# Expert outputs of the last pairs summed by one-hot products in SBUF instead of by accumulating row scatters to DRAM

## The chip, the cores and the metric

The kernel runs on one core of a Trainium2 chip. The metric is the device time of one execution in microseconds (us). Before the change three runs gave 815.13 us as their median (812.78 to 815.39).

The core's engines each run an instruction stream of their own: TensorE (PE in the profile; PEld is its weight load), VectorE (DVE), ScalarE (ACT), GpSimdE (POOL) and SyncE (SP), which here only issues DMAs. Matrix products accumulate in PSUM banks of 128 x 512 f32. Transfers from DRAM run on 16 DMA engines, whoever issues them.

## The reference

One decoder layer over 512 tokens of width 1024: three token mixers (a causal pooling mixer, latent attention, attention into 256 memory tokens) merged by gates, then a mixture of experts and a final RMSNorm. The change lies in the experts and the end. Cut to that part:

```python
def hierarchical_moe(h, w_rg, b_rg, w_re, b_re, w_gate_e, w_up_e, w_down_e):
    ...                                  # top-1 group of 4, top-2 of its 8 experts, weights per token
    def run_block(args):
        toks, e = args
        xb = x_pad[toks]
        a = jax.nn.silu(xb @ w_gate_e[e]) * (xb @ w_up_e[e])
        return a @ w_down_e[e]           # 1024 -> 256 -> 1024
    yb = lax.map(run_block, (row_tok.reshape(n_blk, MOE_BLOCK), blk_e))
    y = yb.reshape(R, D) * row_w[:, None].astype(yb.dtype)
    out = jax.ops.segment_sum(y, row_tok, num_segments=T + 1)[:T]
    return out.reshape(B, S, D)
...
x = x + hierarchical_moe(h2, ...)
return rms_norm(x, final_norm_g)
```

All is float32. There are 32 experts, so 1024 choices of a token and an expert, 32 to an expert on average.

## The kernel before

The first 520 us or so compute the mixers and the router. They are the same in both kernels. Behind them comes the expert stage.

**Pairs and slots.** The 32 experts are taken in 16 pairs (class `Pair`, objects `PP[0]` to `PP[15]`). A pair has 128 slots, 64 (`CAP`) for each of its two experts, and a slot holds one token. `onehot` makes `P`, a 0/1 matrix of tokens by slots; `info` multiplies by it to get each slot's weight (`wt`), its row scale (`rs`) and its token number. An expert with more than 64 tokens sets `flag`, and a branch on it (`tc.If`) runs `overflow`; with the timed inputs the branch is not taken.

**A pair's work.** `fetch` gathers the pair's rows of x from a DRAM copy `xd` (GpSimdE, an indirect DMA). `turn_x` turns them by TensorE, and ScalarE copies them with a scale. `up(0)` to `up(7)` multiply by the gate and up weights; the two experts use the two column halves of the PE array at once. `up(7)` ends with Silu on ScalarE and a product on VectorE. `turn` transposes the 128 x 256 result. `down` multiplies by the down weights in two halves of 512 columns, weighs the rows by `wt` into a tile `y`, and adds `y`'s rows to a DRAM copy of x, `xo`, by an indirect DMA with `compute_op=add` (line 1145), once for each pair. Unused slots point past the end and are dropped.

**The order.** All engines follow one hand-written list of steps for each pair (`SEQ0` for the first, `SEQM`, `SEQL` for the last): U is `up`, x `turn_x`, t and D are the turn and the `down` of the pair before, o, j and f prepare a pair three ahead. I call D(n) the down product of pair n; it stands in the list of pair n + 1.

**The weights.** 192 pieces of 512 KiB (twelve to a pair) are loaded by SyncE into a ring of 40 buffers made of tiles of several tags (`e`, `r`, `wh`, `wl`, `m`, `ac`; the three places of `m` are filled by two DMAs of 256 KiB each). A piece is issued when the one 40 back is used, and not before the DMA eight back has landed. In the list of the last pair the down weights of pair 14 come before the gate and up weights of pair 15, and the down weights of pair 15 last.

**The end.** In pair 14's list (`R`) `ACC` (all 512 rows, four tiles of 128) and `xa` (the rows of pair 14's slots) are read from `xo` behind the scatter of pair 13. `all_rows` norms `ACC` and writes it to the output; the rows of pairs 14 and 15 are not complete there. The rows of pair 14's slots (`xa`) get its product, are normed and written over by slot. For pair 15 the order is longer: its rows can be read (`rows_in(xs, q.ix)`, line 1258) only when the scatter of pair 14 is done; then its own product is added, and the normed rows are written over the output by slot (line 1353). The branch for `overflow` (line 1334) stands between the turn and the down product of pair 15.

Of the kernel before, what the change touches and what calls it, by code (L numbers as in the profile page):

```python
# [41 lines left out]
def trunk_and_moe(ctx, tc, a, out):  # L42
# [1018 lines left out]
    class Pair:
        def __init__(self, p, cd, inf, wts=None):
            self.cd, self.inf, self.wts, self.xe = cd, inf, wts, []
            self.XG = XG[p % 2]
# [42 lines left out]
        def info(self):  # L1107
# [6 lines left out]
            self.it, self.rs, self.wt = it, it[:, 8:9], it[:, 9:10]  # L1114

        def up(self, k):
# [5 lines left out]
            if k == KD - 1:  # L1122
                self.a = ut((128, 512))
                s.activation(self.a[:, 0:256], gu[:, 0:256], AF.Silu, scale=self.rs)
                v.scalar_tensor_tensor(self.a[:, 0:256], gu[:, 256:512], self.rs, self.a[:, 0:256], op0=OP.mult, op1=OP.mult)
# [8 lines left out]
        def down(self, xs=None):  # L1134
            y = ct2()
            for hf in range(2):
                hs = slice(hf * 512, (hf + 1) * 512)
                ps = self.down_half(hf)
                if hf:
                    v.tensor_scalar(y[:, hs], ps, self.wt, None, op0=OP.mult)  # L1140
                else:
                    s.activation(y[:, hs], ps, AF.Copy, scale=self.wt)
                if xs is not None:
                    v.scalar_tensor_tensor(xs[:, hs], ps, self.wt, xs[:, hs], op0=OP.mult, op1=OP.add)
            g.indirect_dma_start(out=xo[:, :], out_offset=bass.IndirectOffsetOnAxis(ap=self.ix[:, :1], axis=0), in_=y, in_offset=None,  # L1145
                                 bounds_check=T - 1, oob_is_err=False, compute_op=OP.add)

        def down_half(self, hf):
            y = bank(PC, "y", 2)
            for k in range(2):  # L1150
                for b, r in enumerate(HALF):
                    pe.matmul(y[r], lhsT=self.aT[:, k, r], rhs=self.wts[b][8 + 2 * k + hf], start=k == 0, stop=k == 1)  # L1152
            return y

# [97 lines left out]
    def rows_in(dst, ix=None):  # L1252

        if ix is None:
            for t in range(4):
                g.dma_start(dst[:, t].rearrange("p a b -> p (a b)"), xo[t * 128:(t + 1) * 128])
        else:
            g.indirect_dma_start(out=dst, out_offset=None, in_=xo[:, :], in_offset=bass.IndirectOffsetOnAxis(ap=ix[:, :1], axis=0),
                                 bounds_check=T - 1, oob_is_err=False)

    def rows_out(src, ix):
        g.indirect_dma_start(out=out[0], out_offset=bass.IndirectOffsetOnAxis(ap=ix[:, :1], axis=0), in_=src, in_offset=None,  # L1262
                             bounds_check=T - 1, oob_is_err=False)

    def norm(x, f):
        s.activation(junk, x, AF.Square, accum_out=f[:, 0:1])
        s.activation(f[:, 1:2], f[:, 0:1], AF.Sqrt, bias=eps[:, 0:1], scale=1.0 / D)
        v.reciprocal(f[:, 2:3], f[:, 1:2])
        v.scalar_tensor_tensor(x, x, f[:, 2:3], gf, op0=OP.mult, op1=OP.mult)

    def all_rows():
        for t in range(4):
            x = ACC[:, t].rearrange("p a b -> p (a b)")
            norm(x, fs[:, t])
            sync.dma_start(out[0, t * 128:(t + 1) * 128], x)
# [4 lines left out]
    fs = cst.tile([128, 6, 4], F32, name="fs")  # L1280
    for p, q in enumerate(PP):
        q.wts = [W[2 * p], W[2 * p + 1]]
        last = p == NP - 1
        for op in (SEQ0 if p == 0 else SEQL if last else SEQM):
            n_ = int(op[1]) if len(op) > 1 else p + 3
            if op[0] == "U":
                q.up(n_)
                if n_ % 2:
                    used(2)
            elif op[0] == "X":  # L1290
# [3 lines left out]
            elif op[0] == "x" and not last:  # L1294
                PP[p + 1].turn_x(n_)
            elif op == "L":
# [14 lines left out]
            elif op == "D":  # L1311
                PP[p - 1].down(xa if last else None)
                used(4)
                if last:
                    rows_in(xs, q.ix)
            elif op == "R" and p == NP - 2:

                gf, xa, xs, o, junk = (wide() for _ in range(5))
                g.memset(xa, 0.0)
                g.memset(xs, 0.0)  # L1320
                g.dma_start(gf, a["final_g"].broadcast_to([128, D]))
                ACC = row_major()
                rows_in(ACC)
                rows_in(xa, q.ix)
            elif op == "N":
                all_rows()
                norm(xa, fs[:, 4])
                rows_out(xa, PP[p - 1].ix)
# [3 lines left out]
    s.activation(f[:, 0:1], eps, AF.Sqrt)
# [1 line left out]
    with tc.If(nc.values_load(flag[0:1, 0:1], min_val=0, max_val=1) > 0):
# [4 lines left out]
    order = tc.manual_schedule()
    order.__enter__()  # L1340
    hs = [slice(hf * 512, hf * 512 + 512) for hf in range(2)]
    for hf in range(2):
# [1 line left out]
        v.scalar_tensor_tensor(xs[:, hs[hf]], ps, q.wt, xs[:, hs[hf]], op0=OP.mult, op1=OP.add)  # L1344
# [3 lines left out]
    v.tensor_tensor(o[:, hs[0]], xs[:, hs[0]], gf[:, hs[0]], op=OP.mult)
# [3 lines left out]
    v.scalar_tensor_tensor(o[:, hs[1]], xs[:, hs[1]], f[:, 3:4], gf[:, hs[1]], op0=OP.mult, op1=OP.mult)  # L1352
# [93 lines left out]
```

## Time and profile before

| what | value |
|---|---|
| median of three runs | 815.13 us |
| the profiled execution: its time | 815.2 us |
| its span, first to last instruction | 813.4 us |
| granted TensorE clock, mean of the span | 0.983 |
| DMA packets, all queues | 167.26 MB |
| PE, DVE, ACT, POOL busy | 94%, 40%, 37%, 36% |

In a timeline row the columns are start and duration in us, engine, source line, operation, written tile <- read tiles, shape, a count where equal instructions follow each other, and in brackets the idle time before the first with what ended it. In a row of stretches there is for each engine the busy time with its instruction count, then the granted TensorE clock (1.00 is full), the busy share of the 16 DMA engines (it can read a little over 1) and the rate in GB/s. One f32 product of 128 x 512 is recorded as two PE records. PE's busy time counts pipelined matmuls with modelled ends, so PE can read as busy while it starves; its waits say more.

### The profile page before, as it was taken

To read this page: it belongs to the slowest core of one execution; us is meant where nothing else is said; L and a number is where in the kernel's file an instruction comes from. 1 tells how busy PE (TensorE), PEld (TensorE's weight loads), DVE (VectorE), ACT (ScalarE), POOL (GpSimd) and SP (SyncE) were. 2 spreads that over 40 slices of the span, in tenths; PEclk is the share of its full clock that TensorE was granted. 3 is DMA by queue.
4 is the path that set the end of the run, shared out by engine and by line. 5 is a ranking of instruction groups with operands and counts; after the bars stand their busy time and mean duration, and the time that the engine had idled before them with its cause. 6 is when DMAs were issued, how large, how long until landed. Compare 5 with 4: busy or idle time off the path is not lost. (4 is left out here: it accounts for less than half of the span.)

```text
span 813.4 us, 9903 instructions
## 1 busy us (share of the span) xinstructions
PE 764.9 (94%) x3629; PEld 512.6 (63%) x3631; DVE 329.3 (40%) x613; ACT 304.0 (37%) x625; POOL 290.3 (36%) x180
## 2 busy tenths in 40 slices
PE   7999999999999999999999999999999998999843
PEld 3778888888887888788888888653333333223200
DVE  5668792344364234677764522423111111100032
ACT  6253453343337353656543322213222232121142
POOL 3255676433332688312226544311121221110301
PEclk9999999999999999999999999999999999999985
DMA  6523333322221322111233499979999999999973
GB/s 221 178 104 104 109 114 141 118 90 79 72 84 31 118 88 71 46 46 56 79 132 130 155 338 342 358 233 355 398 367 403 391 374 378 378 348 393 398 281 127
DMA packets 54371, 167.26 MB, mean 206 GB/s; under 512 B 8396, under 2 KB 9548, under 8 KB 54320
## 3 DMA queue, kind: packets, MB, share of 16 engines
q1 hardware_dynamic: 45792, 149.14, 49.5%
q0 software_dynamic: 5936, 13.01, 5.5%
q10 hardware_dynamic: 2592, 4.46, 1.5%
q8 instruction: 29, 0.48, 0.2%
q14 instruction: 22, 0.18, 0.1%
HBM read 159.86 MB, written 15.20 MB: 215 GB/s over the span
## 5 line engine op out<-in xcount | busy, mean ns | idle before, releaser
L125 POOL TENSOR_TENSOR wl<-r,wh 128x1024 fp32r<-128x1024 f32 (+3 forms) x75 | 167.3, 2238 | 211.0 <-ACT wh L180 187.0
L1121 PE MATMUL gu<-e,u 128*64 128x512 f32 x336 | 92.3, 608 | 3.2 <-DMA e<-in_w_e 3.2
L180 ACT CAST wh<-r 128x1024 fp32r<-128x1024 f32 (+3 forms) x85 | 82.1, 972 | 33.5 <-PE mm L199 13.3
L1145 POOL DMA_INDIRECT xo<-y,ix x15 | 24.0, 1601 | 182.4 <-DVE ix L1079 126.3
L198 PE MATMUL mm<-g,wh 128*128 128x512 f32 x180 | 72.8, 405 | 0.0
L199 PE MATMUL mm<-g,wh 128*128 128x512 f32 x180 | 71.0, 395 | 0.0
L1104 ACT ACTIVATE u<-xe,PR 128x128 f32<-128x128 f32 x120 | 34.2, 368 | 67.6 <-PE xe L1100 67.5
L471 PE MATMUL mm<-box,wh 128*128 128x512 f32 x144 | 56.8, 394 | 0.9 <-ACT wh L180 0.9
L472 PE MATMUL mm<-box,wh 128*128 128x512 f32 x144 | 56.3, 391 | 0.0
L1140 DVE TENSOR_SCALAR y<-y,it 128x512 f32<-128x512 f32 x15 | 11.3, 750 | 110.9 <-PE y L1152 110.9
L201 PE MATMUL mm<-g,wl 128*128 128x512 f32 x180 | 53.5, 395 | 0.0
L1121 PEld LDWEIGHTS gu<-e,u 128*64 128x64 f32 x336 | 24.0, 136 | 39.6 <-issue 23.4
L1152 PE MATMUL y<-e,u 128*64 128x512 f32 x144 | 39.9, 602 | 6.0 <-DMA e<-in_w_e 5.4
L435 ACT ACTIVATE m<-s,st 128x256 f32<-128x256 f32 (+3 forms) x48 | 24.3, 508 | 54.6 <-DVE st L433 54.1
L201 PEld LDWEIGHTS mm<-g,wl 128*128 128x128 f32 x180 | 33.7, 187 | 8.4 <-POOL wl L125 0.2
L198 PEld LDWEIGHTS mm<-g,wh 128*128 128x128 f32 x180 | 34.0, 189 | 7.4
L199 PEld LDWEIGHTS mm<-g,wh 128*128 128x128 f32 x180 | 33.8, 188 | 7.2
L476 PE MATMUL mm<-box,wl 128*128 128x512 f32 x144 | 36.6, 389 | 0.0
L198 PE MATMUL mm<-box,wh 128*128 128x512 f32 x78 | 31.7, 406 | 0.3 <-DVE g L283 0.3
L471 PEld LDWEIGHTS mm<-box,wh 128*128 128x128 f32 x144 | 27.1, 188 | 6.7 <-ACT wh L180 1.3
L476 PEld LDWEIGHTS mm<-box,wl 128*128 128x128 f32 x144 | 27.0, 188 | 5.7
L199 PE MATMUL mm<-box,wh 128*128 128x512 f32 x78 | 30.4, 390 | 0.0
(354 smaller groups left out, 1561.1 us busy)
## 6 DMA issues: line engine op xcount, KB each, us to landing
e<-in_w_e SPq DMA_DIRECT2D x120, 512.0 KB
r<-in_w_in SPq DMA_DIRECT2D x37, 512.0 KB
ac<-in_w_e SPq DMA_DIRECT2D x16, 512.0 KB
r<-in_w_e SPq DMA_DIRECT2D x15, 512.0 KB
wh<-in_w_e SPq DMA_DIRECT2D x15, 512.0 KB
wl<-in_w_e SPq DMA_DIRECT2D x14, 512.0 KB
m<-in_w_e SPq DMA_DIRECT2D x24, 256.0 KB
r<-in_w_bpm SPq DMA_DIRECT2D x8, 512.0 KB
```

What stands on the lines that cost most here:

```text
L125: eng.tensor_tensor(lo, x, hi.bitcast(F32), op=OP.subtract)
L180: s.copy(hi[:, :cols], r[:, :cols])
L198: pe.matmul(ps, lhsT=lh, rhs=rh, start=start and i == 0, stop=False)
L199: pe.matmul(ps, lhsT=lh, rhs=rl, start=False, stop=False)
L201: pe.matmul(ps, lhsT=ll, rhs=rh, start=False, stop=stop and i == m - 1)
L435: s.activation(P[:, :w], S[:, :w], AF.Exp, bias=st4[:, 0:1], accum_out=st4[:, 1:2])
L471: pe.matmul(ps, lhsT=lh, rhs=rh, start=k == 0, stop=False)
L472: pe.matmul(ps, lhsT=lh, rhs=rl, start=False, stop=False)
L476: pe.matmul(ps, lhsT=ll, rhs=rh, start=False, stop=k == KD - 1)
L1104: s.activation(x[:, j], ps[:, j], AF.Copy, scale=PR[:, k:k + 1])
L1121: pe.matmul(gu[r], lhsT=self.xe[k // 4][:, k % 4, r], rhs=self.wts[b][k], start=k == 0, stop=k == KD - 1)
L1152: pe.matmul(y[r], lhsT=self.aT[:, k, r], rhs=self.wts[b][8 + 2 * k + hf], start=k == 0, stop=k == 1)
```

## The change

Pairs 0 to 8 (`SC = 9`) are added to `xo` as before. Behind the down product of pair 8, in the list of pair 9, `xo` is read back to SBUF as `ACC`, into the place where x stood before (tag `ac`), four DMAs of 512 KiB. From pair 9 on nothing is scattered:

- `down` writes the weighted rows as two float32r tiles, high part (ScalarE) and remainder (VectorE).
- `where` makes `PT`, the 0/1 matrix of slots by tokens, from the slots' token numbers (VectorE).
- `combine(i, q)`, i from 0 to 7, multiplies one tile of 128 tokens of `PT` by one half of both parts (two float32r products of 128 x 128 by 512, PSUM bank `xe` or the new bank `cb`) and adds the bank to that part of `ACC` (VectorE). The eight calls of a pair wait in `todo` and are taken at the eight `c` of `SEQM`: four behind its D, four in the next list. Those of pair 13 are finished ahead of the last pair's list, those of pair 14 behind it.

The branch for `overflow` moves from behind the last pair's turn to ahead of the last pair's list. For the last pair `rs * wt` takes the place of `rs` on the up half, so its down product comes weighted. Its rows of `ACC` are picked by products with `P` (eight f32 products of 128 x 128 by 512) into the same two PSUM banks in which its down product then accumulates. All rows of `ACC` are normed and written by SyncE, and the last pair's slots are normed out of PSUM and written over by one scatter, which waits for those four writes. `rows_in`, `rows_out`, `norm`, `all_rows` and `xa`, `xs` go. From its third turn on the ring of weights has 36 buffers, since the four of `ac` hold `ACC`.

```diff
     def place(i):
-        j = i % RING
+        j = i % RING if i < 2 * RING else (i - 2 * RING) % (RING - 4)
...
+        def where(self):
+            tk = cst.tile([128, 4], F32, tag="tk", name=nm("tk"), bufs=1)
+            v.tensor_scalar(tk, K[:, C_TILE:C_TILE + 4], self.it[:, 6:7], -1.0, op0=OP.subtract, op1=OP.mult)
+            self.PT = ut((128, 4, 128), F32R)
+            v.tensor_tensor(self.PT, toks, tk.unsqueeze(2).broadcast_to([128, 4, 128]), op=OP.is_equal)
...
-        def down(self, xs=None):
-            y = ct2()
+        def down(self):
+
+            y = self.y = [ct2()] if self.scattered else [ct2(F32R), ct2(F32R)]
             for hf in range(2):
                 hs = slice(hf * 512, (hf + 1) * 512)
                 ps = self.down_half(hf)
...
+                if not self.scattered:
+                    s.activation(y[0][:, hs], ps, AF.Copy, scale=self.wt)
+                    v.scalar_tensor_tensor(y[1][:, hs], ps, self.wt, y[0][:, hs].bitcast(F32), op0=OP.mult, op1=OP.subtract)
...
+    def combine(i, q):
+        t, hs = i // 2, slice((i % 2) * 512, (i % 2) * 512 + 512)
+        cb = bank(PC, "cb", 1) if i % 2 else bank(PC, "xe", 2)
+        for j in range(2):
+            pe.matmul(cb, lhsT=q.PT[:, t], rhs=q.y[j][:, hs], start=j == 0, stop=j == 1)
+        dst = ACC[:, t].rearrange("p a b -> p (a b)")[:, hs]
+        v.tensor_tensor(dst, dst, cb, op=OP.add)
...
-    SEQM = "o U0 U1 j U2 t U3 x0 D U4 n U5 x1 U6 f U7 R".split()
-    SEQL = "t D U0 U1 N U2 U3 U4 U5 U6 U7".split()
+    SEQM = "o U0 c U1 j c U2 c t c U3 x0 D n U4 w c U5 c x1 c U6 f c U7".split()
+    SEQL = "t D U0 U1 U2 U3 U4 U5 U6 U7".split()
...
+                if p == SC:
+                    ACC = row_major()
+                    for t in range(4):
+                        g.dma_start(ACC[:, t].rearrange("p a b -> p (a b)"), xo[t * 128:(t + 1) * 128])
+                if p > SC:
+                    todo += [lambda i=i, q=PP[p - 1]: combine(i, q) for i in range(8)]
...
+    ys = [bank(PC, "y", 2) for hf in range(2)]
+    for t in range(4):
+        x = ACC[:, t].rearrange("p a b -> p (a b)")
+        todo.pop(0)()
+        todo.pop(0)()
+        if t == 1:
+            q.turn()
+        for hf in range(2):
+            pe.matmul(ys[hf], lhsT=q.P[:, t].bitcast(F32), rhs=x[:, hs[hf]], start=t == 0, stop=False)
+        f = fs[:, t]
+        s.activation(junk, x, AF.Square, accum_out=f[:, 0:1])
+        s.activation(f[:, 1:2], f[:, 0:1], AF.Sqrt, bias=eps[:, 0:1], scale=1.0 / D)
+    for hf in range(2):
+        q.down_half(hf, ys[hf])
+    for t in range(4):
+        x = ACC[:, t].rearrange("p a b -> p (a b)")
+        v.reciprocal(fs[:, t, 2:3], fs[:, t, 1:2])
+        v.scalar_tensor_tensor(x, x, fs[:, t, 2:3], gf, op0=OP.mult, op1=OP.mult)
+        sync.dma_start(out[0, t * 128:(t + 1) * 128], x)
```

How this moves instructions is read from the two programs. **GpSimdE, from the scatter of pair 8 to the end, before** (`xo<-y` is a pair's scatter, `<-xd` a fetch):

```order
L1145 DMA xo<-y_5724,ix_5361 512x1024
L1084 DMA y_4607<-xd,ix_5770 128x1024
L1145 DMA xo<-y_5828,ix_5464 512x1024
L1084 DMA XB<-xd,ix_5872 128x1024
L1145 DMA xo<-y_5929,ix_5566 512x1024
L1084 DMA y_4607<-xd,ix_5973 128x1024
L1145 DMA xo<-y_6030,ix_5667 512x1024
L1084 DMA XB<-xd,ix_6074 128x1024
L1145 DMA xo<-y_6111,ix_5770 512x1024
L1145 DMA xo<-y_6171,ix_5872 512x1024
L1319 MEMSET e_6209 128x1024
L1320 MEMSET e_6210 128x1024
```

And the same engine **now**, from the same scatter to the branch:

```order
L1158 DMA xo<-y_5719,ix_5361 512x1024
L1341 DMA ACC_5743<-xo 128x1024 x4
L1087 DMA y_4607<-xd,ix_5774 128x1024
L1087 DMA XB<-xd,ix_5895 128x1024
L1087 DMA y_4607<-xd,ix_6032 128x1024
L1087 DMA XB<-xd,ix_6171 128x1024
L1290 DMA y_4607<-in_final_g 128x1024
L1295 TENSOR_LOAD flag
```

Five scatters between the fetches and the loads of `xo` behind them are gone, and the four reads of `xo` stand right behind pair 8's scatter, ahead of the fetch for pair 12. **TensorE, in the list of pair 12 behind D(11), now** (`gu` products are `up`, `cb` and `xe` from `y` are `combine`, `xe` from `XB` is `turn_x`):

```order
L1131 MATMUL gu_6052<-wl_5756,u_6021 64x512
L1131 MATMUL gu_6052<-m_5758,u_6021 64x512
L1174 MATMUL xe_6139<-y_6109,u_6000 128x512
L1174 MATMUL xe_6139<-y_6110,u_6000 128x512
L1131 MATMUL gu_6052<-wl_5756,u_6021 64x512
L1131 MATMUL gu_6052<-m_5759,u_6021 64x512
L1174 MATMUL cb_6151<-y_6109,u_6000 128x512
L1174 MATMUL cb_6151<-y_6110,u_6000 128x512
L1103 MATMUL xe_6155<-K,XB 128x128 x4
L1174 MATMUL xe_6165<-y_6109,u_6000 128x512
L1174 MATMUL xe_6165<-y_6110,u_6000 128x512
```

Before, only the `gu` rows and `turn_x` stood there. **TensorE behind the last `up` product, now**, the first two of four tiles (`y<-ACC,P` picks the last pair's rows):

```order
L1174 MATMUL xe_6694<-y_6653,u_6357 128x512
L1174 MATMUL xe_6694<-y_6654,u_6357 128x512
L1174 MATMUL cb_6698<-y_6653,u_6357 128x512
L1174 MATMUL cb_6698<-y_6654,u_6357 128x512
L1356 MATMUL y_6692<-ACC_5743,P_6050 128x512
L1356 MATMUL y_6693<-ACC_5743,P_6050 128x512
L1174 MATMUL xe_6706<-y_6653,u_6357 128x512
L1174 MATMUL xe_6706<-y_6654,u_6357 128x512
L1174 MATMUL cb_6710<-y_6653,u_6357 128x512
L1174 MATMUL cb_6710<-y_6654,u_6357 128x512
L1140 MATMUL at_6714<-K,u_6686 128x128 x2
L1356 MATMUL y_6692<-ACC_5743,P_6050 128x512
```

Before, only the turn, the branch and the eight down products of 64 x 512 stood between the last `up` product and the end; now the branch is past, and sixteen `combine` products and eight picking products come first.

More of the change, by code (lines that the diff above doesn't have):

```diff
@@ L693, in load @@
             i = ring["loaded"]
-            if i % RING == RING - 4 and upto < min(i + 4, len(pieces)):
+            if i == 2 * RING - 4 and upto < i + 4:
                 return
@@ L701, in used @@
         ring["used"] += n_
-        load(ring["used"] + RING)
+        load(max(min(ring["used"] + RING, 3 * RING - 4), ring["used"] + RING - 4))
     def proj_v(p, half, w):
@@ L1150, in down_half @@
+            if self.scattered:
+                g.indirect_dma_start(out=xo[:, :], out_offset=bass.IndirectOffsetOnAxis(ap=self.ix[:, :1], axis=0), in_=y[0], in_offset=None,
+                                     bounds_check=T - 1, oob_is_err=False, compute_op=OP.add)
+        def down_half(self, hf, y=None):
+            more = y is not None
+            if not more:
+                y = bank(PC, "y", 2)
             for k in range(2):
                 for b, r in enumerate(HALF):
-                    pe.matmul(y[r], lhsT=self.aT[:, k, r], rhs=self.wts[b][8 + 2 * k + hf], start=k == 0, stop=k == 1)
+                    pe.matmul(y[r], lhsT=self.aT[:, k, r], rhs=self.wts[b][8 + 2 * k + hf], start=k == 0 and not more, stop=k == 1)
@@ L1161, in trunk_and_moe @@
+    PP = [Pair(p, pairs(code)[:, :, p], None, scattered=p < SC) for p in range(NP)]
     for q in PP[:3]:
@@ L1242, in overflow @@
                     q.down()
+                    for i in range(8):
+                        combine(i, q)
     SEQ0 = "X0 b1 X1 b2 X2 U0 X3 U1 X4 U2 X5 U3 X6 U4 X7 U5 j0 o U6 j1 x0 U7 L x1 j2 j f".split()
-    SEQM = "o U0 U1 j U2 t U3 x0 D U4 n U5 x1 U6 f U7 R".split()
-    SEQL = "t D U0 U1 N U2 U3 U4 U5 U6 U7".split()
[L1252 to L1275, printed above, removed]
+    SEQM = "o U0 c U1 j c U2 c t c U3 x0 D n U4 w c U5 c x1 c U6 f c U7".split()
+    SEQL = "t D U0 U1 U2 U3 U4 U5 U6 U7".split()
+    todo = []
+    fs = cst.tile([128, 5, 4], F32, name="fs")
     def wide():
         return W0.tile([128, 2, T], F32, tag="e0", name=nm("e"), bufs=6).rearrange("p a b -> p (a b)")
-    fs = cst.tile([128, 6, 4], F32, name="fs")
     for p, q in enumerate(PP):
@@ L1283, in trunk_and_moe @@
         last = p == NP - 1
+        if p == NP - 2:
+            gf = XG[0]
+            g.dma_start(gf, a["final_g"].broadcast_to([128, D]))
+        if last:
+            while todo:
+                todo.pop(0)()
+            order.__exit__(None, None, None)
+            with tc.If(nc.values_load(flag[0:1, 0:1], min_val=0, max_val=1) > 0):
+                extra[0] = True
+                overflow()
+                extra[0] = False
+            order = tc.manual_schedule()
+            order.__enter__()
+            q.rw = fs[:, 0, 3:4]
+            v.tensor_tensor(q.rw, q.rs, q.wt, op=OP.mult)
         for op in (SEQ0 if p == 0 else SEQL if last else SEQM):
@@ L1295, in trunk_and_moe @@
                 PP[p + 1].turn_x(n_)
+            elif op == "w" and SC <= p < NP - 1:
+                q.where()
             elif op == "L":
@@ L1311, in trunk_and_moe @@
             elif op == "D":
-                PP[p - 1].down(xa if last else None)
+                PP[p - 1].down()
                 used(4)
[L1314 to L1328, printed above, removed]
```

53 lines of the change are left out of this document (22 added, 31 removed).

## The prediction

> **What bounds the kernel now.** The trunk is untouched, so I read the expert stage and the end. First the table of stretches:
>
> ```profile
> core 0: us, PE busy (x) PEld busy (x) DVE busy (x) ACT busy (x) POOL busy (x), PEclk, DMA share, GB/s
> 676.50:784.90 108.40, 91.07 (x323) 28.45 (x322) 8.64 (x23) 26.70 (x69) 16.77 (x16) 0.98 1.00 379
> 677.00:690.00 13.00, 10.65 (x44) 3.36 (x40) 1.89 (x4) 3.05 (x9) 2.63 (x2) 1.00 1.02 408
> 690.00:694.00 4.00, 4.00 (x16) 1.30 (x14) 0.54 (x4) 0.37 (x1) 0.00 (x0) 1.00 1.05 332
> 746.00:750.00 4.00, 3.65 (x15) 1.01 (x12) 0.00 (x0) 0.37 (x1) 0.00 (x0) 1.00 1.05 320
> 648.00:660.00 12.00, 11.91 (x58) 4.12 (x56) 1.90 (x4) 3.81 (x11) 2.63 (x2) 1.00 0.99 372
> 717.00:729.00 12.00, 11.69 (x47) 3.94 (x46) 1.29 (x3) 2.53 (x7) 2.63 (x2) 1.00 0.92 303
> ```
>
> The DMA engines are full (share 1.00) and move about 408 GB/s where only loads and gathers run. Then the timeline of PE, at products with down weights (L1152) and at the last `up`:
>
> ```profile
> 637.09 3.65 PE L1152 MATMUL y<-e,u 128*64 128x512 f32 x16
> 650.21 3.65 PE L1152 MATMUL y<-e,u 128*64 128x512 f32 x16
> ...
> 676.45 1.08 PE L1152 MATMUL y<-e,u 128*64 128x512 f32 x4
> 678.87 1.07 PE L1152 MATMUL y<-e,u 128*64 128x512 f32 x2 [1.34 <-DMA e<-in_w_e]
> ...
> 695.39 1.04 PE L1152 MATMUL y<-e,u 128*64 128x512 f32 x2 [0.34 <-DMA e<-in_w_e]
> ...
> 713.94 1.07 PE L1152 MATMUL y<-r,u 128*64 128x512 f32 x2
> ...
> 784.85 0.64 PE L1121 MATMUL gu<-r,u 128*64 128x512 f32 x1 [1.44 <-DMA r<-in_w_e]
> 785.33 0.59 PE L1121 MATMUL gu<-r,u 128*64 128x512 f32 x1
> 785.76 1.02 PE L1121 MATMUL gu<-r,u 128*64 128x512 f32 x2
> ```
>
> While the ring holds weights, a pair takes PE 650.21 - 637.09 = 13.1 us. At D(9), 676.45, the ring is empty; from there PE waits for weights and a pair takes 18.9, then 18.55 us. **Until the last `up` product ends at 785.76 + 1.02 = 786.8 (call it E), the DMA engines are the bound**, with about 5 us of a pair's time free on PE. Behind E come 26.6 us of a chain:
>
> ```profile
> 785.11 0.75 DVE L1144 SCALAR_TENSOR_TENSOR e<-y,it,e 128x512 f32<-128x512 f32 x1 [22.67 <-DMA e<-xo,ix]
> 787.10 0.15 DVE L1268 RECIPROCAL fs<-fs 128x1 f32<-128x1 f32 x1
> 787.28 1.64 POOL L1145 DMA_INDIRECT xo<-y,ix  x1 [15.78 <-DVE fs L1268]
> 788.49 0.16 DVE L1268 RECIPROCAL fs<-fs 128x1 f32<-128x1 f32 x1
> ...
> 795.09 1.04 POOL L1258 DMA_INDIRECT e<-xo,ix  x1 [6.17 <-DMA xo<-y,ix]
> ...
> 797.00 0.20 ACT L1332 ACTIVATE fs<-eps 128x1 f32<-128x1 f32 x1
> 797.30 0.18 PEld L1152 LDWEIGHTS y<-r,u 128*64 128x64 f32 x1 [2.42 <-ACTq L1334]
> ...
> 801.36 0.75 DVE L1344 SCALAR_TENSOR_TENSOR e<-y,it,e 128x512 f32<-128x512 f32 x1 [6.82 <-DMA e<-xo,ix]
> ...
> 805.62 0.75 DVE L1352 SCALAR_TENSOR_TENSOR e<-e,fs,e 128x512 f32<-128x512 f32 x1
> 807.18 1.00 POOL L1262 DMA_INDIRECT out_dram<-e,ix  x1 [7.18 <-DVE e L1352]
> ```
>
> A gather of rows lands at 785, the scatter of pair 14 leaves at 787, its rows come back at 801, the result is ready at 806.4, and its scatter and the end take 813.4 - 806.4 = 7.0 us.
>
> **The change: what leaves the DMA stream.** The scatters of pairs 9 to 13 fall between D(9) and E:
>
> ```profile
> L1145 POOL DMA_INDIRECT xo<-y,ix x7 | 11.2, 1601 | 102.7 <-DVE ix L1079 54.8 <-DVE y L1140 32.2 <-DVE fs L1268 15.8
> ```
>
> These seven from 663 us on are pairs 8 to 14; 8 stays and 14 comes behind E. What one costs the stream: in 108.4 us 379 x 108.4 = 41.1 MB moved. 67 pieces of 0.524 MB landed in that time, 35.1 MB; three gathers and `xa` at 64 rows of 4 KB (1024 choices over 16 pairs) are 1.05, `xo` 2.1, the gain 0.5. 2.35 MB are left, 0.47 a scatter: read and written. That is 0.47/0.408 = 1.15 us. Besides, the rate sinks about each: 690 to 694 loses 4 x (1 - 332/408) = 0.75 us. So 1.9 us each, 9.5 for five; bounds from the rows: 0.75 (the dip alone), and 2.5 (18.55 less the 16 us that twelve pieces and a gather take at 408). With `xa` gone (0.26 MB, 0.6 us) the last gate weights land **10.1 us earlier**. The four reads of `xo` move from 768 to about 677; the bytes are the same, so E doesn't move by them, but D(10) comes 2.1/0.408 = 5.1 us later and 1.9 earlier: 695.4 + 3.2 = 698.6.
>
> One thing is added. With 36 buffers the `m` places, half-size DMAs of which eight may be out, hold pieces 149 to 151 (before 153 to 155) and once more 185 to 187, the last three that `up` needs. Loading them before, the stream thinned: 717 to 729 loses 12 x (1 - 303/408) - 0.75 = 2.3 us, but 648 to 660 only 0.3. I take **1.3**, halfway, and keep both ends. So weights put E at 786.8 - 10.1 + 1.3 = 778.0.
>
> **What is added on PE, and its cover.**
>
> ```profile
> 482.53 0.39 PE L883 MATMUL mm<-a,wh 128*128 128x512 f32 x1
> 482.76 0.39 PE L884 MATMUL mm<-u,wh 128*128 128x512 f32 x1
> ...
> 538.79 1.16 PE L1093 MATMUL xe<-P,ACC 128*128 128x128 f32 x8
> ```
>
> A float32r product of this shape records 0.39 us but starts 0.23 after the one ahead, which is its cost; the upper bound is 0.39. A pair has sixteen: 3.7 us, and PE needs 13.1 + 3.7 = 16.8 a pair, where weights come every 18.55 - 1.9 = 16.65. **PE and DMA become level**; the cover is used up. From 698.6, D(13) is at 749.0. Then come 9.4 us of products (3.5 down, 3.5 `up`, 0.6 turn, 1.8 `combine`).
>
> ```profile
> L1144 DVE SCALAR_TENSOR_TENSOR e<-y,it,e 128x512 f32<-128x512 f32 x2 | 1.5, 746 | 22.7 <-DMA e<-xo,ix 22.7
> L1125 DVE SCALAR_TENSOR_TENSOR u<-gu,it,u 128x256 f32<-128x256 f32 x7 | 3.4, 483 | 23.6 <-ACT u L1124 23.6
> L1348 DVE TENSOR_TENSOR e<-e,e 128x512 f32<-128x512 f32 x1 | 0.7, 683 | 0.0
> L1269 DVE SCALAR_TENSOR_TENSOR ACC<-ACC,fs,e 128x1024 f32<-128x1024 f32 x4 | 5.1, 1285 | 0.1
> ```
>
> Ahead of the branch PE must let VectorE finish: Silu, its product (0.48) and four adds of 0.75 take 4.1 us, then the turn and copy 1.0. (Adds that wait hold PSUM banks; with two of `xe` and one of `cb` a bank is asked for again after two products of `up` or `turn_x`, 1.5 to 2 us, and an add takes 0.75.) The branch itself, before: ACT's last instruction ends at 797.20 and PE goes on at 797.30 behind it, so 0.1 us; the bound is 2.0, from PE's own turn that ended at 795.3. D(14) is at 749.0 + 14.6 = 763.6, and with 3.5 + 6.9 us PE would reach E at 774.0. Weights say 778.0: 4 us of slack. SyncE's part of the branch waits for all loads to land, but behind it stand only the output writes. VectorE's adds (8 x 0.75 a pair) and `where` (0.7) leave it half idle. The waiting reads of `xo` hold the fetch of pair 12 on POOL from 670 to about 679; it is used at 698.
>
> **The end.** Behind E: `combine` of a tile takes PE 0.9 us and VectorE 2 x 0.75; picking a half waits for its add and takes 0.86: two records that start 0.43 apart (785.33, 785.76), as for a product on half the columns. The nearest full-width rows, at 538.79, take 1.16/8 = 0.145 for a quarter of the width, weight load included, so the upper bound is 8 x 0.145 = 1.16 a product and +2.4 us for eight. Tile by tile the last add ends at E + 11.7, the last picking at 12.7, the down products at 16.1. VectorE norms four tiles at 1.39 (787.10 to 788.49): 17.2. Two products with the gain, the factor, the scale: 19.6. But the scatter also waits for the four writes:
>
> ```profile
> out_dram<-e,ix POOLq DMA_INDIRECT x2, 3.3
> ACC<-xo POOLq DMA_DIRECT2D x4, 512.0 KB, 10.0
> ```
>
> The last write leaves at 17.2; 0.26 MB landed in 3.3 us unloaded, 0.52 MB need 0.6 more: 21.1 (10.0 in a full stream is the upper end, but weights are gone then). With 0.4 us to start and 807.18 to 813.4 behind, the end is E + 27.7; before it was 26.6. **The tail is 1.1 us longer**, though two DRAM round trips have gone.
>
> **Sum.** 778.0 + 27.7 = 805.7 against a span of 813.4: -7.7. The profiled execution took 815.2, 1.8 more than its span, and the median is 815.13; so I forecast **807.5 us**.
>
> **A rule weighed.**
>
> ```profile
> 734.00:739.50 5.50, 5.43 (x15) 2.28 (x17) 0.00 (x0) 0.69 (x1) 0.00 (x0) 0.69 1.03 411
> 790.00:800.00 10.00, 3.39 (x10) 1.14 (x12) 4.43 (x7) 2.33 (x4) 2.05 (x2) 0.50 0.82 278
> ```
>
> The granted clock falls to half at the end of before, where PE is mostly idle, and also in the stage, behind waits of only 1.5 us. The Trainium skill (TensorE: Matmul & The Clock Gate, "What's actually happening") has the clock halve after an idle window of about 3.4 us; by that the new tail, whose longest gap is 1 us, stays at full speed and gains over the old one, which the sum already has. The trace at 734 shows a drop on less, so I keep the drop as a rival.
>
> **Rivals.**
> 1. *PE at half clock behind E* (the slower side). Place: the products behind E; condition: a drop in the starved last 8 us. Every PE step doubles, the down products end at E + 29.6, the result is ready 2.1 later, and with 7.0 behind it the end is 11 us later: 818.5. It decides from 10 us on, that is only if the half clock lasts nearly the whole tail. Against it: at 782 to 787, more starved, the clock was full. 7%; half as long, 811 to 814, 5%.
> 2. *PE becomes the bound*, `combine` costing its recorded 0.39: 19.4 a pair, D(13) at 756.8, with 2.7 more behind it E at 784.5, time 814; a part of this, or a longer stop at the branch, 811 to 814. Against it: the 0.23 between rows. 12%.
> 3. *The scatters hid in the stream*, and weights come no earlier: E stays, tail +1.1: 816.2. Against it: the dips at each scatter. 5%.
> 4. *Better*: little thinning at `m`, scatters at 2.5 us; PE's own 774.0 is then the floor: 774.0 + 27.7 + 1.8 = 803.5. 10%.
>
> The forecast itself, 804.5 to 811, gets 61%. Three tenths of a per cent, 812.7 to 817.6, is about what can be told from no change. Faster: 61 + 10 + 9 of the 17 between = 80%; the same 12; slower 8, nearly all rival 1. Range **803 to 814**, which the bounds of the scatter (0.75 to 2.5 us) also give.
>
> **What would show it.** D(10) at about 698.6 and then periods near 16.7; PE's waits from there nearly gone; E at 778; no dip at scatters; the second `m` epoch by a thinner stream just ahead of E; clock 1.00 behind E; the last `combine` add at E + 11.7 and the final scatter at E + 21.5, ended by a write's landing. I am wrong if E lies beyond 783, by PE rows without waits (rival 2) or with them (rival 3), or if the tail exceeds 31 us.

## The result and the profile after

| | before | after |
|---|---|---|
| median of five runs | 813.10 us (812.42 to 815.39) | 807.81 us (805.84 to 810.23) |
| the profiled execution: time, span | 815.2, 813.4 us | 807.81, 806.0 us |
| granted TensorE clock, mean of the span | 0.983 | 0.991 |
| DMA packets, all queues | 167.26 MB | 164.17 MB |
| PE, DVE, ACT, POOL share of the span busy | 94%, 40%, 37%, 36% | 97%, 45%, 38%, 34% |

The ratio after to before is 0.9928, 95% interval 0.9901 to 0.9954: faster by 0.7%, or about 5.9 us; the medians differ by 5.3. The forecast was 807.5 us, 7.6 below the 815.13 it started from. **The sum came out right by luck: two of its parts were wrong and cancelled**, as the trace shows. All medians and ratios leave out two executions in a slow state, one of e9 (1692.58 us) and one of before taken beside e9 to e11 (856.97 us).

The stretches of the trace of after that answer to those of before (columns as there: each engine's busy time, the granted clock, the DMA share, GB/s):

```profile
672.40:779.30 106.90, 102.30 (x408) 36.01 (x407) 44.70 (x81) 23.87 (x62) 6.85 (x9) 0.97 0.95 369
677.00:690.00 13.00, 11.68 (x44) 3.83 (x40) 6.54 (x12) 2.30 (x6) 1.72 (x2) 1.00 1.03 410
712.00:724.00 12.00, 12.00 (x55) 4.83 (x54) 5.76 (x11) 4.03 (x11) 0.00 (x0) 1.00 0.94 326
754.00:764.00 10.00, 8.80 (x36) 3.60 (x32) 6.97 (x12) 2.08 (x6) 0.00 (x0) 1.00 1.03 404
762.00:766.00 4.00, 1.46 (x5) 0.58 (x4) 2.00 (x4) 0.37 (x1) 0.00 (x0) 0.85 1.04 389
766.00:770.00 4.00, 3.96 (x10) 1.23 (x12) 0.00 (x0) 0.15 (x1) 0.00 (x0) 0.50 1.04 398
770.00:774.00 4.00, 4.00 (x17) 1.17 (x14) 1.50 (x2) 1.22 (x2) 0.00 (x0) 0.80 0.51 203
774.00:779.00 5.00, 5.00 (x26) 1.54 (x22) 0.00 (x0) 0.00 (x0) 0.00 (x0) 1.00 0.00 0
```

In the last two rows the stream ends: it is half empty from 770 on and moves nothing from 774 on, and PE works on without a pause. The timeline of PE and its weight loads (PEld) in the same trace, with the down products (L1167), a `combine` call (L1174), the turn (L1140) and the last `up` products (L1131):

```profile
672.39 1.08 PE L1167 MATMUL y<-e,u 128*64 128x512 f32 x4
696.00 4.33 PE L1167 MATMUL y<-e,u 128*64 128x512 f32 x15
696.70 0.36 PEld L1167 LDWEIGHTS y<-e,u 128*64 128x64 f32 x2 [0.50 <-DMA e<-in_w_e]
697.97 0.20 PEld L1167 LDWEIGHTS y<-e,u 128*64 128x64 f32 x4 [0.92 <-DMA e<-in_w_e]
715.05 0.64 PE L1167 MATMUL y<-r,u 128*64 128x512 f32 x1
732.55 3.65 PE L1167 MATMUL y<-e,u 128*64 128x512 f32 x16
750.05 3.65 PE L1167 MATMUL y<-e,u 128*64 128x512 f32 x16
762.77 0.73 PE L1174 MATMUL cb<-y,u 128*128 128x512 f32 x2 [0.70 <-DVE ACC L1176]
764.92 0.66 PE L1140 MATMUL at<-K,u 128*128 128x128 f32 x2 [1.42 <-DVEq L1295]
766.04 1.11 PE L1167 MATMUL y<-r,u 128*64 128x512 f32 x1 [0.46 <-ACT u L1142]
777.01 2.31 PE L1131 MATMUL gu<-m,u 128*64 128x512 f32 x9
```

E is 777.01 + 2.31 = 779.3, and no `up` product of the last pair waits for a DMA: **PE sets E, not the weights**, which were there some 5 us earlier (the stream's last four pieces are down weights, which no `up` product needs). Ahead of D(14) PE waits for an add, for VectorE's part of the branch (L1295) and for the turn's copy, and then runs at half clock: a product that records 0.59 us elsewhere records 1.11.

The end, from VectorE, GpSimdE and (third row) the chain of waits:

```profile
790.57 0.68 DVE L1176 TENSOR_TENSOR ACC<-ACC,cb 128x512 f32<-128x512 f32 x1
795.61 1.28 DVE L1365 SCALAR_TENSOR_TENSOR ACC<-ACC,fs,y 128x1024 f32<-128x1024 f32 x1
796.92 2.65 DMA out_dram<-ACC
800.44 1.02 POOL L1377 DMA_INDIRECT out_dram<-e,ix  x1 [59.74 <-DMA out_dram<-ACC]
```

The last add ends at E + 11.9, the norms at E + 17.6, the last write lands at E + 20.3, the scatter behind it leaves at E + 21.1, and the span ends at E + 26.7.

Set against the forecast, both counted from D(9), which is 676.45 before and 672.39 after:

| from D(9) to | forecast | after | off by |
|---|---|---|---|
| D(10) | 22.1 | 23.6 | +1.5 |
| D(13) | 72.6 | 77.7 | +5.1 |
| D(14) | 87.2 | 93.7 | +6.5 |
| E, by PE | 97.6 | 106.9 | +9.4 |
| E, by the weights | 101.6 | not later than about 102 | |
| end | 129.3 | 133.6 | +4.3 |

From D(9) on the forecast had 7.7 us of gain; the trace has 136.95 - 133.6 = 3.3. The rest of the profiled difference, 4.1 us, lies ahead of D(9), all of it ahead of D(0), where the change adds and removes nothing. In the time of the trace that the forecast was made against, E would lie at 676.45 + 106.9 = 783.4, beyond the 783 that the forecast had named as a sign of being wrong.

### The profile page after: what moved, and what is told of

Read it like the earlier page. It is cut to its first block, busy times and chain, and to the rows that moved or that the text cites. A ratio compares the mean times of both kernels' runs of the same rounds, so it can differ in the third digit from the quotient of the medians.

```text
span 806.0 us, 10157 instructions
## 1 busy us (share of the span) xinstructions
PE 779.0 (97%) x3741; PEld 524.1 (65%) x3743; DVE 365.8 (45%) x675; ACT 304.4 (38%) x626; POOL 276.8 (34%) x169
## 2 busy tenths in 40 slices
DMA packets 53509, 164.17 MB, mean 204 GB/s; under 512 B 7906, under 2 KB 9058, under 8 KB 53456
## 5 line engine op out<-in xcount | busy, mean ns | idle before, releaser
L1131 PE MATMUL gu<-e,u 128*64 128x512 f32 x336 | 88.8, 607 | 0.9 <-DMA e<-in_w_e 0.9
L198 PE MATMUL mm<-g,wh 128*128 128x512 f32 x180 | 71.9, 400 | 0.0
L199 PE MATMUL mm<-g,wh 128*128 128x512 f32 x180 | 70.2, 390 | 0.0
L471 PE MATMUL mm<-box,wh 128*128 128x512 f32 x144 | 56.8, 394 | 0.9 <-ACT wh L180 0.9
L472 PE MATMUL mm<-box,wh 128*128 128x512 f32 x144 | 56.3, 391 | 0.0
L1158 POOL DMA_INDIRECT xo<-y,ix x9 | 14.3, 1594 | 89.9 <-DVE ix L1082 79.7
L1131 PEld LDWEIGHTS gu<-e,u 128*64 128x64 f32 x336 | 20.4, 135 | 33.0 <-issue 26.1
L1167 PE MATMUL y<-e,u 128*64 128x512 f32 x160 | 38.9, 600 | 0.4 <-DMA e<-in_w_e 0.4
L198 PE MATMUL mm<-box,wh 128*128 128x512 f32 x78 | 31.7, 406 | 0.5 <-DVE g L283 0.5
L471 PEld LDWEIGHTS mm<-box,wh 128*128 128x128 f32 x144 | 27.1, 188 | 6.7 <-ACT wh L180 1.3
L1154 DVE TENSOR_SCALAR y<-y,it 128x512 f32<-128x512 f32 x9 | 6.8, 751 | 54.1 <-PE y L1167 54.1
L472 PEld LDWEIGHTS mm<-box,wh 128*128 128x128 f32 x144 | 27.1, 188 | 5.3
```

The source lines that it names most:

```text
L198: pe.matmul(ps, lhsT=lh, rhs=rh, start=start and i == 0, stop=False)
L199: pe.matmul(ps, lhsT=lh, rhs=rl, start=False, stop=False)
L471: pe.matmul(ps, lhsT=lh, rhs=rh, start=k == 0, stop=False)
L472: pe.matmul(ps, lhsT=lh, rhs=rl, start=False, stop=False)
L1131: pe.matmul(gu[r], lhsT=self.xe[k // 4][:, k % 4, r], rhs=self.wts[b][k], start=k == 0, stop=k == KD - 1)
```

## The experiments

One table for all runs. D(0) is the first down product; ahead of it the change adds and removes nothing.

| run | median, us (lowest to highest) | ratio to before, 95% | D(0) | D(0) to E | E to end | D(0) to end |
|---|---|---|---|---|---|---|
| before | 813.10 (812.42 to 815.39) | 1 | 558.0 | 228.8 | 26.6 | 255.4 |
| after | 807.81 (805.84 to 810.23) | 0.9901 to 0.9954 | 553.9 | 225.4 | 26.7 | 252.1 |
| e1 | 802.03 (801.36 to 802.38) | 0.9849 to 0.9882 | 555.3 | 219.6 | 24.6 | 244.2 |
| e2 | 803.41 (803.05 to 804.42) | 0.9868 to 0.9902 | 553.5 | 221.7 | 26.0 | 247.7 |
| e3 | 807.44 (803.77 to 808.29) | 0.9904 to 0.9944 | 553.6 | 224.8 | 26.7 | 251.5 |
| e4 | 808.23 (807.34 to 810.16) | 0.9930 to 0.9960 | 553.6 | 225.3 | 26.7 | 252.0 |
| e5 | 806.56 (805.48 to 808.00) | 0.9902 to 0.9947 | 555.3 | 221.4 | 27.1 | 248.4 |
| e6 | 806.26 (804.33 to 808.52) | 0.9892 to 0.9933 | 553.9 | 223.9 | 26.7 | 250.6 |
| e7 | 806.27 (804.05 to 810.06) | 0.9893 to 0.9932 | 558.0 | 220.0 | 30.4 | 250.3 |
| e8 | 803.06 (801.36 to 808.67) | 0.9855 to 0.9893 | 560.1 | 227.5 | 19.3 | 246.8 |
| e9 | 804.80 (801.88 to 806.07) | 0.9864 to 0.9935 | 553.5 | 219.8 | 26.7 | 246.6 |
| e10 | 799.36 (797.11 to 804.39) | 0.9791 to 0.9841 | 558.5 | 223.9 | 20.3 | 244.1 |
| e11 | 814.30 (one run) | | 557.1 | 228.5 | 26.9 | 255.4 |
| e12 | 813.08 (809.05 to 816.31) | 0.9977 to 1.0011 | 553.2 | 227.9 | 26.1 | 254.0 |

### What a scatter costs the stream (e1)

The kernel before, with the scatters of five pairs left out:

```diff
+            if self in PP[9:14]:
+                return
             g.indirect_dma_start(out=xo[:, :], ..., compute_op=OP.add)
```

> The kernel before, with the scatters of pairs 9 to 13 left out (their sums are missing in the output) and nothing put in their place. If a scatter costs the full DMA stream 1.9 us, as the prediction had it, E (the end of the last up product) comes 9.5 us earlier than in the kernel before and the time is 803 to 804.5 us. If only the dips cost (0.75 us each), 809.3. If the scatters hid in the stream, 813. The tail behind E keeps its 26.6 us by all three.

D(9), the last gate and up weights' wait, and the last `up` row in the trace of e1:

```profile
673.74 2.17 PE L1154 MATMUL y<-e,u 128*64 128x512 f32 x4
772.96 0.64 PE L1121 MATMUL gu<-r,u 128*64 128x512 f32 x1 [1.04 <-DMA r<-in_w_e]
773.87 1.02 PE L1121 MATMUL gu<-r,u 128*64 128x512 f32 x2
```

Here PE still waits for a DMA just ahead of E, so the stream sets it. D(9) to E takes 774.9 - 673.7 = 101.2 us, 110.3 in before, 110.1 in its second trace (e11) and 109.5 in e12, whose expert stage is the same: 8.4 to 9.2 us, **1.7 to 1.8 us a scatter**; 1.9 was forecast. The timed median fell by 10.9, to 802.03, below the 803 to 804.5 expected: the tail, which was expected to stay, is 2.0 us shorter. In it the last rows of `xo` are there 13.6 us behind E (14.6 in before), and the last down products run at full clock (at 0.50 in before); how much each is worth stays open.

### Who sets E in the changed kernel (e2, e6, e4)

```diff
-        for j in range(2):
-            pe.matmul(cb, lhsT=q.PT[:, t], rhs=q.y[j][:, hs], start=j == 0, stop=j == 1)
+        pe.matmul(cb, lhsT=q.PT[:, t], rhs=q.y[0][:, hs], start=True, stop=True)
```

> The kernel after, where combine multiplies the high part of y alone (the remainder part of the sums is left out): half of its products, the DMAs as they are. If PE sets E from D(10) on (the new theory, from the trace of after), PE has 8 x 0.27 = 2.2 us a pair less, E moves from 779.3 to where the weights allow it, 774 to 776, and the tail loses about 2 more: 801 to 803 us. If the weights set E, as the prediction had it, E stays and only the tail gains: 805.5 to 806.

Same DMAs, less PE work, and D(0) to E is 3.7 us shorter, the median 4.4 us lower. That is the first theory's result, though the median misses its range by 0.4; by the second E would have stayed. So PE sets E. Of the 3.7 us, 1.1 lie behind D(14), where the half clock lasted 3.5 us here and 6.9 in after; from D(10) to D(14) e2 is 4.2 us shorter, and its step to D(10) is 1.7 longer.

e6 and e4 are one number, `SC = 8` and `SC = 10`.

> The kernel after with SC = 8: one scatter less, eight combine calls more. Theory 1: PE starves between D(9) and D(11) (the stream sets those two) and is the bound only behind them. Then the 4.4 us of the added combine calls fall into that starved time, D(10) or D(11) comes one scatter (1.9 us) earlier, and so does E: 805.5 to 806.5 us. Theory 2: PE is the bound of the whole stretch; then E is 4.4 us later: 811 to 812.5. Theory 3: the weights set E: 806 too, but with PE waiting for DMA ahead of E.

> The kernel after with SC = 10: one pair more is scattered, one less combined. If PE sets E, PE has 4.4 us less to do and the stream one scatter more (about 1.9 us): E at 775 to 776.5, time 804 to 805.5 us. If the weights set E, E comes 1.9 us later: 809.5 to 810.

D(8), D(9), D(10) and D(11) in e6:

```profile
659.22 0.64 PE L1167 MATMUL y<-r,u 128*64 128x512 f32 x1
678.81 3.81 PE L1167 MATMUL y<-e,u 128*64 128x512 f32 x16
696.91 3.65 PE L1167 MATMUL y<-e,u 128*64 128x512 f32 x16
714.86 0.64 PE L1167 MATMUL y<-r,u 128*64 128x512 f32 x1
```

In after the first two steps take 13.2 and 23.6 us, here 19.6 and 18.1: the added `combine` work went into time in which PE starved, and D(13) lies 196.0 us behind D(0), in after 196.1. From 696.91 to 714.86, 17.95 us, is a pair with its eight calls where PE doesn't starve; without them it took 13.1, so a call costs 4.8 / 8 = **0.60 us**. (The pairs from D(11) on have no `info` step ahead and take 17.5.) The theory that PE is the bound of the whole stretch falls. The time, 806.26, is the one that the first theory gave, but not for its reason: the scatter's 1.9 us didn't come out ahead of D(13), since with eight more calls PE has little starved time left, and most of what E gained (1.2 of 1.5 us) came behind D(14), where the half clock lasted 3.5 us instead of 6.9. Neither e6's median nor e4's can be told apart from after's. e4 missed its 804 to 805.5: D(9) to D(10) fell to 18.5, but with the reads of `xo` a list later D(10) to D(11) rose to 25.5, and 44.0 us together are more than after's 42.7. **What `SC` moves between PE and the stream comes back on the other side.**

### The branch and the half clock (e3, e5, e7)

e3 puts the last four `combine` calls of pair 13 behind the branch:

```diff
-    SEQL = "t D U0 U1 U2 U3 U4 U5 U6 U7".split()
+    SEQL = "c c t c c D U0 U1 U2 U3 U4 U5 U6 U7".split()
...
-            while todo:
-                todo.pop(0)()
```

> The kernel after, where the last four combine calls of pair 13 stand behind the branch, two ahead of the turn and two behind it, where PE stood still. If PE sets E, the stop shrinks by about 2 us, and if the half clock behind the branch came from the stop, 3 more: E at 774.5 to 777, time 803 to 805.5 us. If the half clock does not depend on the stop, 805.5 to 806. If the weights set E, no change: 807.8.

PE behind the branch, and D(14), in e3:

```profile
764.10 0.84 PE L1174 MATMUL xe<-y,u 128*128 128x512 f32 x2 [1.95 <-DVEq L1293]
764.74 1.06 PE L1174 MATMUL cb<-y,u 128*128 128x512 f32 x2
767.86 0.66 PE L1167 MATMUL y<-r,u 128*64 128x512 f32 x1
```

A miss (803 to 805.5 expected, 807.44 measured). The stop is as long as before, since the first product behind the branch waits for VectorE too, and the half clock falls on the `combine` calls (1.06 us instead of 0.63). D(14) to E is 10.5 instead of 13.3 us, but D(9) to D(10) took 26.4 here, and E moved by 0.6.

e5 leaves the branch out:

> The kernel after without the branch for overflow (left out; it is not taken with these inputs). If the stop at the branch costs what the trace of after shows, the turn behind it comes 1.5 us earlier, and if the stop also set off the half clock (2.9 us in D(14) and the first up products), D(14) to E takes 10.4 instead of 13.3 us: E at about 775 in the time of the profile of after, 803.5 to 804.5 us. If the half clock comes from something else there, 806.3.

From D(13) to E it takes 24.9 us, 29.3 in after: 4.4 less, as much as expected, though not in the parts expected. The granted clock is 1.00 all the way, and the turn comes 3.0 us earlier instead of 1.5, since the last `combine` call with its 0.70 us wait no longer stands ahead of it; that call now runs among the products of D(14), and D(14) to E takes 12.2 us, not 10.4. The median fell by only 1.3 us; its D(0) is 1.3 us later than in after, which leads to e12.

e7 puts the branch between `up(3)` and `up(4)` of the last pair, with the calls of pair 13 around the turn:

> The kernel after with the branch between up(3) and up(4) of the last pair, where VectorE has nothing open, and the last four combine calls of pair 13 around the turn in its old place. If the stop came from VectorE being held by Silu and the product ahead of the branch, PE stands 1 us or less there and the clock stays full: D(14) 2.8 us earlier, E at 775 to 776, 803.5 to 804.5 us. If the branch itself stops PE for 2 us wherever it stands, with the half clock behind it, nothing is gained: 807 to 808.

D(0) to E is 5.4 us shorter than in after, more than expected. But the tail is 3.6 us longer, and the median, 806.27, lies between the two forecasts. PE in e7 behind the last `up`:

```profile
780.10 0.73 PE L1174 MATMUL xe<-y,u 128*128 128x512 f32 x2 [2.16 <-ACTq L1317]
781.62 3.35 PE L1355 MATMUL y<-ACC,P 128*128 128x512 f32 x4 [0.32 <-DVE ACC L1176]
```

The wait has only moved: `up` products pass behind the branch, the first product that reads another engine's work from ahead of it waits (ACTq L1317 is ScalarE's part of the branch), and the half clock comes behind that (3.35 us for what takes 1.98).

### The calls in twos (e9)

In the trace of after a `combine` call is dear on the way from one kind of product to the other. PE there, starts in the first column:

```profile
757.73 1.08 PE L1131 MATMUL gu<-e,u 128*64 128x512 f32 x4
758.74 0.73 PE L1174 MATMUL cb<-y,u 128*128 128x512 f32 x2
759.40 1.08 PE L1131 MATMUL gu<-e,u 128*64 128x512 f32 x4
760.41 0.73 PE L1174 MATMUL xe<-y,u 128*128 128x512 f32 x2
760.99 0.62 PE L1174 MATMUL cb<-y,u 128*128 128x512 f32 x2
761.45 0.62 PE L1174 MATMUL xe<-y,u 128*128 128x512 f32 x2
```

One call between two `up` steps takes 759.40 - 758.74 = 0.66 us, and the step ahead of it 1.01 where it takes 0.86 in a row; the second of two calls in a row takes 761.45 - 760.99 = 0.46, which is the forecast's 2 x 0.23.

```diff
-    SEQM = "o U0 c U1 j c U2 c t c U3 x0 D n U4 w c U5 c x1 c U6 f c U7".split()
+    SEQM = "o U0 c c U1 j U2 c c t U3 x0 D n U4 w U5 c c x1 U6 c c f U7".split()
```

> The kernel after with the same combine calls taken two by two (cc) instead of one between two up products. In the trace of after a combine call between up products takes 0.81 us of PE (0.15 on the way in, 0.66 on the way out), the second and third in a row 0.58 and 0.46: it is the change of kind that costs. If so, a pair takes 0.9 us less where PE is the bound (17.5 to 16.6 us from D(11) on), E comes 2.5 to 3 us earlier, 804.5 to 805.5 us. If a call costs the same wherever it stands, 807.8; if two in a row wait for VectorE's adds to free their banks, a pair takes more and the time is 808 to 810.

D(12), D(13), the call ahead of the branch, the turn behind it and D(14) in e9, then a stretch of it:

```profile
730.66 3.65 PE L1167 MATMUL y<-e,u 128*64 128x512 f32 x16
747.46 3.65 PE L1167 MATMUL y<-e,u 128*64 128x512 f32 x16
759.83 0.74 PE L1174 MATMUL cb<-y,u 128*128 128x512 f32 x2 [0.70 <-DVE ACC L1176]
761.98 0.41 PE L1140 MATMUL at<-K,u 128*128 128x128 f32 x2 [1.42 <-DVEq L1295]
762.86 0.64 PE L1167 MATMUL y<-r,u 128*64 128x512 f32 x1 [0.46 <-ACT u L1142]
```

```profile
762.00:766.00 4.00, 3.54 (x18) 1.30 (x20) 0.36 (x1) 1.06 (x2) 0.00 (x0) 1.00 1.03 375
```

A pair takes 16.8 us instead of 17.5: 0.7 us gained, 0.9 expected. And the stop at the branch has the same waits as in after to a hundredth (0.70, 1.42, 0.46), but **this time the clock stays at 1.00**. E comes 5.6 us earlier in the trace: 2.8 behind D(14), where the clock is full, the rest ahead of it, which is the 2.5 to 3 expected of the calls.

### All that helped together (e8, e10)

e8 is `SC = 8`, the branch of e7, and the eight calls of pair 14 among the `up` products of the last pair; e10 has `SC = 9`, the calls in twos, and no call close ahead of the branch (`B`):

```diff
+    SEQL = "c c t c c D U0 U1 c c U2 U3 B U4 U5 c c U6 c c U7 c c".split()
```

> The kernel after with SC = 8, the branch as in the run before, and the eight combine calls of pair 14 among the up products of the last pair instead of behind them (PE does them before E, so E comes 4.4 us later than without, but the tail loses 5 to 6 us, among it VectorE's adds that PE waits for, and its output writes leave earlier). By theory 1 of PE: 1.9 from SC, 3 from the branch, 1 to 2 from the tail, so 801 to 802.5 us. If E is held by the weights by then, the combine calls cost nothing ahead of E: 799 to 801. If neither the branch nor SC helps, 806 to 808.

> The kernel after with all that has helped: SC = 9, combine calls two by two, the last four of pair 13 around the turn, the branch between up(3) and up(4) of the last pair with no combine call close ahead of it (so VectorE and ScalarE have nothing open there), and the combine calls of pair 14 among the up products of the last pair. From the traces, D(0) to the end: 252.1 us in after, 246.8 in e8; 2.5 to 4 less than e8 by the calls in twos and a shorter stop at the branch, so 243 to 244.5 and a time of 799 to 800.5 us. If the stop at the branch or the half clock stay, 801 to 803.

PE behind the branch, the last pair's down products and the final scatter in e10:

```profile
778.02 0.70 PE L1174 MATMUL xe<-y,u 128*128 128x512 f32 x2 [0.49 <-PEq L1317]
790.47 3.65 PE L1167 MATMUL y<-e,u 128*64 128x512 f32 x16
797.02 1.02 POOL L1374 DMA_INDIRECT out_dram<-e,ix  x1 [51.67 <-ACT e L1372]
```

The stop is 0.49 us, the clock stays full, and the final scatter waits for its own rows and no longer for an output write. e10 takes **799.36 us, ratio 0.9816 (0.9791 to 0.9841)**: it beats both kernels, and time and stage (244.1 us from D(0)) are as expected. e8 was expected at 801 to 802.5 and took 803.06.

### What lies ahead of D(0) (e11, e12)

> The kernel before once more, unchanged, for a second trace of it. From D(0) to the end the first trace takes 255.4 us, and D(0) lies at 558.0, where the nine other traces have 553.5 to 560.1. If the expert stage repeats and the time ahead of D(0) is what varies, D(0) to the end is 255.4 within 0.7 us here, wherever D(0) lies. If the stage itself varies by some us, not.

255.4 again, with D(0) 1.0 us earlier: the expert stage of before repeats, and the time ahead of it varies. (e12, with the same stage, has 254.0.) One reason for the variation is on record in the granted clock: near 535 us it is halved for 3.5 us in before, e11, e7 and e10, for 6.9 us in e8, and not at all in the other traces. From the first product of L883 (L884 in the changed kernels) to D(0) it takes 94.9 to 95.1 us with the short stretch, 96.6 with the long one and 93.3 to 93.5 without. It comes and goes in kernels of either sort, and from run to run of one kernel the mean clock differs alike (e8: 0.987 in the traced run, 0.996 to 0.998 in the five others), so it doesn't come from the change.

> The kernel before with one more small constant tile (16 bytes a partition, one memset), which moves every tile behind the constants by 32 bytes of SBUF, as the tile tk of the change does. Ahead of D(0), which the change does not touch, the traces fall into two groups: between the first product of L550 and the first scores of the heads (L746 before, L747 after) 155.7 us in before, its second trace, e1 and e5; 154.1 to 154.2 in after and the other seven; and between L770 (L771) and L883 (L884) 115.5 against 114.6. Where the tiles stand splits them the same way: wh starts at byte 62400 in before and e1 and 62144 in e5, both multiples of 64, and at 62432 in after. If the place of the tiles sets the pace of the products there, this kernel shows 154.1 and 114.6 and takes 2.5 us less than before: 810.3 to 811.3. If it is something else in the program, 155.7 and 115.5, and 813.

```diff
     fs = cst.tile([128, 6, 4], F32, name="fs")
+    pad = cst.tile([128, 4], F32, name="pad")
+    v.memset(pad, 0.0)
```

The same float32r products in before, then in e12, and behind each the start of L746:

```profile
320.10 0.39 PE L199 MATMUL mm<-g,wh 128*128 128x512 f32 x1
320.33 0.40 PE L198 MATMUL mm<-g,wh 128*128 128x512 f32 x1
320.57 0.39 PE L199 MATMUL mm<-g,wh 128*128 128x512 f32 x1
...
330.18 0.39 PE L746 MATMUL s<-g,g 128*128 128x512 f32 x1
```

```profile
320.27 0.39 PE L198 MATMUL mm<-g,wh 128*128 128x512 f32 x1
320.50 0.39 PE L199 MATMUL mm<-g,wh 128*128 128x512 f32 x1
320.72 0.39 PE L198 MATMUL mm<-g,wh 128*128 128x512 f32 x1
...
327.73 0.39 PE L746 MATMUL s<-g,g 128*128 128x512 f32 x1
```

The products start 0.233 us apart in before and 0.227 in e12, and both stretches read 154.1 and 114.5 us, as in after. So **32 bytes in the place of the tiles change the pace of these products by 2.6%**, 2.5 us in all. But the median of e12, over twelve runs, is only 0.5 us below before's, within the interval of no change; the one trace is the fastest of the twelve. Part of the answer is the granted clock on record for each run: its mean is 0.983 over these twelve and 0.985 over the seventeen runs of before beside them. A straight line through time against clock for both, an estimate, puts e12 1.6 us below before at the same clock (standard error 0.5). Why these runs had the lower clock no trace here shows.

## Why the forecast was right, and where it wasn't

- **Scatters in the stream: right.** 1.7 to 1.8 us each (e1) against 1.9. The chain "PE rows with waits for DMA up to E" was a true reading of before.
- **The thinner stream at `m`: too large, harmless.** 1.3 us were taken for the second epoch; from 754 to 764 the stream moved 404 GB/s, so it is nearly nothing, the lower bound. From 712 to 724 it thinned as before did a little later.
- **"4 us of slack" on PE: the step that failed.** The forecast had PE at 97.6 us behind D(9) and the weights at 101.6; PE came at 106.9. Five terms make the 9.4 us:
  - D(10): the reads of `xo` net of a scatter were worked out at 3.2 us; 4.7 in after (18.9 to 23.6). Undersized by 1.5; in e2, e3, e5, e7, e9 and e10, which read `xo` at the same place, the step took 23.1 to 26.4 in all, so it varies by some 3 us.
  - `combine`: 0.23 a product holds only behind another of its kind. With the change of kind a call costs 0.60 us (e6), a pair 4.8 instead of 3.7. From D(10) to D(11) that is 1.1; from D(11) to D(13), whose pairs lack an `info` step of 0.45 us, 0.7 a pair (17.5 against 16.8): 2.5 in all.
  - PE still starved behind D(10), where the forecast let it run freely: the step to D(11) took 19.05 us, 1.1 more than the 17.95 of e6; PE's weight loads for D(10) waited 0.5 and 0.9 us for DMAs.
  - The stop at the branch: 16.0 instead of 14.6, 1.4 more. The sum had it at VectorE's finish plus the turn; the branch's own passing (PE's 1.42 us wait for VectorE) was bounded at 2.0 and taken as 0.1.
  - The half clock, granted from 764.8 to 771.7: 2.9 us behind D(14). It was a rival, but put behind E. There the clock stayed full up to PE's last product, as the forecast said.
- **The tail: nearly right, 1.0 too long.** 11.9, 17.6, 20.3 and 21.1 us behind E against 11.7, 17.2, 21.1 and 21.5; the rest of the miss is the stretch from the scatter to the end, 5.6 instead of 6.2 us.
- **The start of the sum: wrong by 4.1 us in the other direction.** The sum was made against the profiled execution of before, whose D(9) lies at 676.45. After has it at 672.39. 2.5 us of that is the pace of the products ahead of D(0) (e12 shows it in its trace); 1.4 lies between there and D(0), where before ran at a mean clock of 0.91 from 520 to 540 and after at 1.00, which doesn't come from the change (e7, e8 and e10 have the half clock too); 0.1 lies ahead of both. The forecast had no term for any of it, so that its number came out is luck.
- **Which rival came true?** A part of the second: PE became the bound, not because `combine` took its recorded 0.39 us, but through starvation, changes of kind and the branch.

On the half clock, the forecast weighed a page against a row. The Trainium skill (TensorE: Matmul & The Clock Gate, "What's actually happening") also says that the window of activity runs freely, so that the point of change varies between runs. The traces agree: after, e6 and e9 stop at the branch with the same waits, 0.70, 1.42 and 0.46 us; the clock is 0.50 for 6.9 us in after and for 3.5 in e6, and stays at 1.00 in e9. A short stop is a risk of a half clock, not its certain cause.

By one trace each the stage is 3.3 us faster (1.9 against that of e12), by the medians the kernel 5.3. The difference lies ahead of D(0). The place of the tiles moves that part by 2.5 us in the traces; the medians of e12 and before differ by 0.5, 1.6 by the estimate at the same clock. How much of the 5.3 the change itself brings stays open.

## What to carry to other kernels

When a bound is lifted, add up the next engine's chain with its waits, not its busy time: work that fills one engine's free 5 us a pair makes it the bound as soon as it starves once and can't catch up. Group products of one kind, keep work that depends on the other engines away from both sides of a branch, and move what can be done earlier out of the tail: e10 has the same scatters and sums as the change and is another 8 us faster. And compare two kernels stage by stage from a common mark: here 4.1 of 7.4 us lay ahead of the first instruction that the change touches.

## What the runs showed of the hardware

- float32r products of 128 x 512 on the same data start 0.227 or 0.233 us apart according to where their tiles stand in SBUF: in the built programs `wh` starts at byte 62432 where it is 0.227, and at 62400 or 62144, multiples of 64, where it is 0.233. All fourteen traces fall in line (154.1 to 154.2 us against 155.7 from L550 to L746, L747 in the changed kernels); which of the shifted tiles does it is not shown.
- A stop of PE of 1.42 us behind one of 0.70 was followed by 6.9 us at half clock in one trace (after), by 3.5 in another (e6) and by none in a third (e9); one of 2.0 us in e1 by none either, one of 1.95 us in e3 by 3.5.
- `up` products pass a branch at once; the first product behind it that needs work of VectorE or ScalarE from ahead of it waits until that engine has passed too: 1.42 us (after), 1.95 (e3), 2.16 (e7). In e10, where nothing was open, it waits 0.49 us, for PE's own part of the branch.
